# A two-layer encoder on one core: split products of 256 columns put side by side into one of 512, and new lengths in the instruction planner

## The chip, the core and the metric

One core of a Trainium2 chip runs the whole program. The metric is the device time of one execution in microseconds. Engine names are those of the profile: PE multiplies matrices, PEld loads its stationary operand, DVE, ACT and POOL compute on vectors, SP only issues DMAs.

## The reference, cut to what matters

512 tokens of 1024 features pass two layers. Each is a half-step FFN, a mixer, an attention into 256 memory tokens and a second half-step FFN, each followed by a layer norm. The first layer's mixer (even) is dense and windowed attention, the second's (odd) is neighbourhood attention. The change touches the projection of the odd mixer's values and that of the memory's keys:

```
def mixer_c(h, w_in, w_out, rpb):              # the odd mixer
    q, k, v = jnp.split(h @ w_in, 3, axis=-1)
    ...
def memory_attn(h, mem, w_q, w_kv, w_o):
    q = (h @ w_q).reshape(B, S, MEM_HEADS, MEM_HEAD_DIM)
    k, v = jnp.split(mem @ w_kv, 2, axis=-1)
    ...
```

## The kernel before, in words

Products are made in a rounded float type (`fp32r`). To keep fp32's precision each operand is split into a high part (`split`: ACT rounds it by a copy) and a low part (DVE subtracts the high part from the source). `mm3` then adds three products in one PSUM bank: high by high, high by low, low by high. A bank holds 512 fp32 columns per partition.

Two places multiply with a moving operand of only 256 columns, three times for each of eight blocks of 128 features:

- `values` in `mixer_c` (the odd mixer): four groups of 256 columns of `c_w_in`, four blocks of 128 token positions each. The stationary operand is the tokens' features (`xh`, `xl`), the moving one is the weights (`w_cols_k`: two halves of 4 x 256, split into a high and a low slab each). The result is split straight out of PSUM. Group 0 stands at the head of the mixer, where the layer norm of the FFN ahead is still in work; groups 1 to 3 stand between the heads' pairs.
- `keys` in `memory`'s `project`: four heads in each of two layers, two blocks of 128 features. The stationary operand is the weights (`w_cols`), the moving one the memory tokens (`self.mt`, split by `memory_tokens`). Both blocks share a bank, and `split_t2` splits it.

The loop of the odd mixer runs over eight pairs of heads. In it, `queries` and `keys` project, split into two `t2` tiles, and copy the parts by DMAs issued on SP (64 x 512 each, eight for a pair's keys, four for its queries) into slabs that hold both parts on 128 partitions. `weights_of` forms the scores from these slabs in banks `a`, and the softmax. `turned` transposes the weights, `attend` multiplies with the values into banks `d`. The even mixer works alike with `scores` (banks `a`), `turned` (transposes into banks `t`) and `attend`, and has projections to interleave (`last_columns`, `share`).

Nothing is issued as it is written. Each operation goes through `Graph.record` (so the profile gives all of them one line, L154), which notes its dependences and a length from `Graph.cost`. `plan` then lays out all engines in time with these lengths: on each engine the ready operation of the lowest key goes first. `deadlines` takes from that a latest start for DVE, ACT and POOL work, and a second `plan` with these as keys gives the order that is emitted. Tiles come from rings of buffers (`t2` 14, `slab` 27, `raw` 2; PSUM banks `a` 3, `d` 2, `t` 3), granted in the order of recording. So a length in `cost`, or the time at which a buffer comes free, moves instructions on all five engines.

Of the kernel before, what the change touches and what calls it, by code (L numbers as in the profile page):

```python
# [12 lines left out]
F32 = mybir.dt.float32  # L13
F32R = mybir.dt.float32r
# [3 lines left out]
ALU = mybir.AluOpType  # L18
AX = mybir.AxisListType

P = 128
D = 1024
S = 512
NT = S // P
KB = D // P
DFF = 2816
MEM = 256
# [38 lines left out]
class Graph:  # L66
# [45 lines left out]
    @staticmethod  # L112
    def cost(engine, method, out, ins, kw):
        n = 1
        for d in (out if method != "tensor_reduce" else ins[0]).ap[1:]:
            n *= d[1]
        wide = any(z.space == bass.MemoryType.PSUM for z in ins + [out]) if engine != "sync" else False
        if method == "dma_start":
            return 1200.0 if "accum_op" in kw else 600.0
        if engine == "tensor":  # L120
            return max(n / 2.4 + 14, 111)
        scalars = sum(1 for z in ins if z.ap[-1][1] == 1)
        if engine == "vector":
            if method == "tensor_scalar" and not wide:
                n = n / 2
            return n / 0.96 + 72 + 60 * scalars + 120 * (method == "scalar_tensor_tensor" and "accum_out" in kw)
        if engine == "scalar":
            return n / 1.2 + (55 if wide else 100) + 45 * scalars + 130 * ("accum_out" in kw)
        if n <= 8:
            return 270.0 if method == "tensor_scalar" else 200.0 if method != "tensor_tensor" else 390.0 + 157.0 * n  # L130
        if method == "memset":
            return n * 0.83 + 60
        dense = len(ins) == 2 and all(z.ap[-1][0] != 0 for z in ins)
        return n * (2.4 if dense else 1.7) + (70 if dense else 130)
# [182 lines left out]
class Kernel:  # L317
# [81 lines left out]
    def w_cols_k(self, w, c0):  # L399

        src = w[:, c0 : c0 + 256].rearrange("(k p) f -> p k f", p=P)
        half = [lambda r, i=i: r[:, 4 * i : 4 * i + 4, :] for i in range(2)]
        return self.weights([(half[i], half[i](src)) for i in range(2)], (KB, 256), half)

    def w_cols512(self, w, c0):

        got = []
        for q in range(2):
            src = w[q * 512 : (q + 1) * 512, c0 : c0 + 512].rearrange("(k p) f -> p k f", p=P)
            got += self.weights(  # L410
                [(lambda r: r, src)], (4, 512), [lambda r, i=i: r[:, 2 * i : 2 * i + 2, :] for i in range(2)]
            )
        return got
# [800 lines left out]
    def mixer_c(self, ln_i, last):  # L1214
        nc, a = self.nc, self.a
        w_in, w_out = a["c_w_in"], a["c_w_out"]
# [3 lines left out]
        def values(grp, t):  # L1220

            if t == 0:
                wv[0] = self.w_cols_k(w_in, 2 * D + 256 * grp)
                vp[grp] = [self.slab(F32R, (P, 2, 4, 2, 64)) for _ in range(2)]
                if grp == 0:
                    for dst, lo in ((slice(64, 128), 0), (slice(0, 64), 448)):
                        nc.scalar.copy(ends[0][:, :, dst], self.xh[:, :, lo : lo + 64])
                        nc.vector.tensor_copy(ends[1][:, :, dst], self.xl[:, :, lo : lo + 64])
            ps = self.ps("t" if grp else "a")
            for k in range(KB):  # L1230
                mv = [z[:, k % 4, :] for z in wv[0][k // 4]]
                x = self.xT(k, 64 + t * P, 64 + (t + 1) * P) if t < 3 else [z[:, k, :] for z in ends]
                self.mm3(ps[:, :256], x, mv, k == 0, k == KB - 1)
            z = vp[grp][t // 2][:, t % 2]
            self.split(ps[:, :256].rearrange("p (v c) -> p v c", v=4), z[:, :, 0], z[:, :, 1])

        def queries(pair, first=False):

# [121 lines left out]
        vp, qs, ks, acts = {}, {}, {}, []  # L1360
        wv, wq, wk, wo = [None], [None], [None], {}
        for t in range(NT):
            values(0, t)
# [32 lines left out]
    def memory_tokens(self):  # L1396

        raw = self.tile(self.raw, [P, KB, MEM], F32, "raw")
        self.nc.sync.dma_start(out=raw, in_=self.a["mem_t"].rearrange("(k p) m -> p k m", p=P))
        self.mt = []  # L1400
        for kk in range(4):
            self.mt.append(self.split_pair(raw[:, 2 * kk : 2 * kk + 2, :].rearrange("p k m -> p (k m)")))

    def memory(self, i, ln_i, last):
        nc, a = self.nc, self.a
        w_q, w_kv, w_o = a["mem_w_q"][i], a["mem_w_kv"][i], a["mem_w_o"][i]
        memT = lambda k, lo, hi: [z[:, (k % 2) * 256 + lo : (k % 2) * 256 + hi] for z in self.mt[k // 2]]

        def project(head):

            got = {}

            def keys():
                wk = self.w_cols(w_kv, 256 * head)
                ps = self.ps("a")
                for b in range(2):
                    for k in range(KB):
                        self.mm3(ps[:, b * 256 : b * 256 + 256], [z[:, k, :] for z in wk[b]], memT(k, 0, 256), k == 0, k == KB - 1)
                got["k"] = self.split_t2(ps)

            def values():
                wv = self.w_cols512(w_kv, D + 256 * head)
                vs.extend(self.pair() for _ in range(2))
                for m in range(2):
                    ps = self.ps("a")
                    for k in range(KB):
                        self.mm3(ps, memT(k, m * P, (m + 1) * P), [z[:, k % 2, :] for z in wv[k // 2]], k == 0, k == KB - 1)
                    for j, both in enumerate(vs):
                        self.split(ps[:, j * 256 : j * 256 + 256], *(z[:, m * 256 : m * 256 + 256] for z in both))

            def queries(b):
                if b == 0:
                    got["w"] = self.w_cols(w_q, 256 * head)
                ps = self.ps("a")
                for lo, hi in [(0, 256), (256, 512)] if head == 0 else [(0, 512)]:
                    self.project(got["w"][b], ps, lo, hi)
                got["q", b] = self.split_t2(ps, scale=-1.0 / 16)

            return got, [keys] + [values] * (head % 2 == 0) + [lambda: queries(0), lambda: queries(1)]

        def weights_of(kt, q):
            p = []
            for tt in range(2):
                ps = self.ps("a")
                for j in range(2):
                    t = 2 * tt + j
                    for b in range(2):
                        self.mm3(
                            ps[:, j * 256 : j * 256 + 256],
                            [z[:, t * P : (t + 1) * P] for z in q[b]],  # L1450
                            [z[:, b * 256 : b * 256 + 256] for z in kt],
                            b == 0,
                            b == 1,
                        )
                mn = self.small(2, "mn2")
                nc.vector.tensor_reduce(out=mn, in_=ps.rearrange("p (j m) -> p j m", j=2), axis=AX.X, op=ALU.min)
                u = self.t2(F32)
                for j in range(2):
                    c = slice(j * 256, j * 256 + 256)
                    self.softmax(u[:, c], P, mn[:, j : j + 1], 0, 256, sums=ps[:, c])  # L1460
                p.append(u)
            return p
# [20 lines left out]
        acts, hs, out, vs = [], [], [], []  # L1483
        got, todo = project(0)
        for f in todo:
            f()
        for head in range(4):
            p, now = weights_of(got["k"], [got["q", b] for b in range(2)]), vs.pop(0)
            todo = []
            if head < 3:  # L1490
                got, todo = project(head + 1)
            if head == 2:
                out = self.staged(self.down_steps(hs, w_o, 0, 256, 1.0 / ALPHA, [], False, alone=True))
# [135 lines left out]
```

## Time and profile before

| | |
|---|---|
| time before | 2140.82 us, median of 3 runs (2138.66 to 2141.06) |
| the profiled execution's own time | 2139.44 us |
| its span, first to last instruction | 2137.6 us |
| PE, share of the span with a matmul in work | 99%, 12904 matmuls |
| DVE, ACT, POOL, shares of the span | 81%, 54%, 13% |
| granted PE clock | 0.998 |

PE's share counts a matmul until its modelled end, and the next starts earlier: a 256-column matmul stands in the record for 0.28 us, while its successor starts 0.12 us after it. So idle time in the record is smaller than the time lost, and starts of matmuls are compared below. Stages are told by time from the span's start: the even mixer from 346 to 590 us, memory to 700, two FFNs to 1393, the odd mixer to 1600, memory to 1780, the last FFN to the end.

### The profile page before, as it was taken

Reading aid. Unit: us, or ns where it says so; the run is one execution under the profiler, and the core shown is the slowest. Engines: PE = TensorE matmul, PEld = TensorE weight load, DVE = VectorE, ACT = ScalarE, POOL = GpSimd, SP = SyncE. Lnnn points to the kernel's source line nnn. Section 1 sums busy time; section 2 is a strip of 40 time slices with the busy share of each in tenths; the row PEclk is TensorE's granted clock in tenths of the full one; section 3 lists DMA queues with packets and bytes.
Section 4 is the critical chain, followed back from the end, with each engine's and each line's share of the span. In section 5 each row is a group of like instructions: output and inputs, shape, how many; then the busy total and the mean of one; then the engine's idle time right before and its main releaser. Section 6 shows DMA issues by size and latency. Waiting matters only on the chain.

```text
span 2137.6 us, 33130 instructions
## 1 busy us (share of the span) xinstructions
PE 2116.6 (99%) x12904; PEld 1886.3 (88%) x12904; DVE 1725.9 (81%) x2460; ACT 1150.2 (54%) x1863; POOL 288.1 (13%) x379
## 2 busy tenths in 40 slices
PE   9999999999999999999999999999999999999997
PEld 7999988788888899999889999888888888999996
DVE  7789989888748879998879999865568479699997
ACT  5555543798446555445545455456665455445552
POOL 0001015310002000000200000412110011000003
PEclk9999999999999999999999999999999999999999
DMA  6566562003443247564445556255354333456551
GB/s 203 142 165 144 139 188 88 21 17 103 138 138 109 83 115 188 148 153 133 139 108 140 127 139 190 72 168 153 104 163 156 127 102 99 109 148 150 140 155 60
DMA packets 208861, 275.96 MB, mean 129 GB/s; under 512 B 10688, under 2 KB 151616, under 8 KB 208704
## 3 DMA queue, kind: packets, MB, share of 16 engines
q1 hardware_dynamic: 175904, 221.14, 33.3%
q0 software_dynamic: 32512, 52.44, 13.7%
q8 instruction: 102, 1.67, 0.3%
q14 instruction: 55, 0.45, 0.1%
q10 hardware_dynamic: 288, 0.26, 0.0%
HBM read 259.12 MB, written 4.19 MB: 123 GB/s over the span
## 4 chain that ended last, share of the span: by engine, by line
PE 72%; DMA 1%; DVE 1%; ACT 1%; SPq 0%; issue 0%; DVEq 0%; ACTq 0%
PE a L154 45%; PE d L154 15%; PE t L154 11%; DMA slab<-t 1%; DVE slab L154 1%; ACT t L154 0%; DVE x L154 0%; SPq L154 0%; DMA raw<-c_w_in 0%; DMA raw<-ab_w_out 0%; ACT slab L154 0%; DVE t L154 0%; DVE xl L154 0%; ACT junk L154 0%; DVEq L1625 0%
## 5 line engine op out<-in xcount | busy, mean ns | idle before, releaser
L154 DVE TENSOR_TENSOR slab<-slab,slab 128x1024 fp32r<-128x1024 f32 (+3 forms) x638 | 728.6, 1168 | 74.9 <-ACT slab L154 35.8
L154 ACT CAST slab<-slab 128x1024 fp32r<-128x1024 f32 (+2 forms) x498 | 472.3, 983 | 338.9 <-DVE slab L154 141.5
L154 PE MATMUL a<-slab,slab 128*128 128x256 f32 (+2 forms) x2456 | 570.5, 315 | 3.9 <-DMA slab<-t 3.4
L154 PE MATMUL a<-xh,slab 128*128 128x256 f32 (+2 forms) x2480 | 560.2, 315 | 0.1
L154 PEld LDWEIGHTS a<-slab,slab 128*128 128x128 f32 x2456 | 417.2, 191 | 37.4 <-issue 2.7
L154 PE MATMUL d<-slab,slab 128*128 128x512 f32 (+2 forms) x1856 | 447.8, 382 | 0.8 <-DVE slab L154 0.5
L154 PEld LDWEIGHTS a<-xh,slab 128*128 128x128 f32 x2480 | 416.9, 191 | 33.6 <-ACT slab L154 1.0
L154 PE MATMUL a<-xl,slab 128*128 128x256 f32 (+1 forms) x1240 | 390.6, 315 | 0.0
L154 PE MATMUL a<-raw,slab 128*128 128x256 f32 x2048 | 388.9, 283 | 0.9 <-DVE t L154 0.7
L154 PEld LDWEIGHTS d<-slab,slab 128*128 128x128 f32 x1856 | 329.2, 189 | 57.6 <-DVE slab L154 1.2
L154 PEld LDWEIGHTS a<-raw,slab 128*128 128x128 f32 x2048 | 328.1, 192 | 6.4 <-ACT slab L154 1.7
L154 PEld LDWEIGHTS a<-xl,slab 128*128 128x128 f32 x1240 | 236.6, 191 | 18.1
L154 PE MATMUL t<-slab,slab 128*128 128x512 f32 (+1 forms) x864 | 209.6, 383 | 0.0
L154 DVE TENSOR_TENSOR slab<-raw,slab 128x1024 fp32r<-128x1024 f32 (+2 forms) x132 | 158.6, 1220 | 23.7 <-ACT slab L154 23.6
L154 PEld LDWEIGHTS t<-slab,slab 128*128 128x128 f32 x864 | 151.4, 189 | 25.1
L154 DVE TENSOR_TENSOR slab<-t,slab 128x512 fp32r<-128x512 f32 (+2 forms) x211 | 131.4, 642 | 29.0 <-ACT slab L154 27.8
L154 ACT CAST slab<-raw 128x1024 fp32r<-128x1024 f32 (+1 forms) x124 | 123.0, 1021 | 25.7 <-PE a L154 9.0
L154 ACT CAST slab<-t 128x512 fp32r<-128x512 f32 (+2 forms) x211 | 114.4, 567 | 41.5 <-PE t L154 13.7
L154 DVE SCALAR_TENSOR_TENSOR x<-d,x 128x512 f32<-128x512 f32 x168 | 114.8, 686 | 18.8 <-PE d L154 18.0
L154 ACT COPY t<-a 128x512 f32<-128x512 f32 x96 | 56.3, 587 | 125.0 <-PE a L154 71.9
L154 POOL DMA_DIRECT2D slab<-ffn_w_down x40 | 47.7, 1193 | 313.5 <-DVE slab L154 291.2
L154 PE MATMUL a<-slab,xh 128*128 128x512 f32 (+1 forms) x272 | 79.8, 375 | 0.5 <-ACT xh L154 0.5
(126 smaller groups left out, 2138.2 us busy)
## 6 DMA issues: line engine op xcount, KB each, us to landing
slab<-ffn_w_gate SPq DMA_DIRECT2D x80, 512.0 KB
slab<-ffn_w_up SPq DMA_DIRECT2D x80, 512.0 KB
slab<-ffn_w_down SPq DMA_DIRECT2D x80, 512.0 KB
slab<-ffn_w_down POOLq DMA_DIRECT2D x40, 512.0 KB, 5.6
raw<-mem_w_kv SPq DMA_DIRECT2D x16, 1024.0 KB
slab<-t SPq DMA_DIRECT2D x96, 128.0 KB
slab<-ffn_w_gate POOLq DMA_DIRECT2D x16, 512.0 KB, 7.8
slab<-ffn_w_up POOLq DMA_DIRECT2D x16, 512.0 KB, 5.8
```

Of the source, the lines that this page charges most:

```text
L154: op.call = lambda: fn(*args, **kw)
```

## The change

`side_step` puts the high and low parts of the moving operand side by side in one slab: one product of 512 columns with the stationary high part fills both halves of a bank (high by high left, high by low right), and one of 256 columns with the stationary low part adds to the left half. `side_sum` copies the right half out (ACT) and adds the left half (DVE), and the split then reads that sum from a `t2` tile instead of PSUM. `w_cols_side` splits the values' weights in four pieces instead of two; `memory_tokens` writes its parts side by side. The memory's keys take a bank `a` for each block of 128 features instead of one for both. In the planner's `cost`, an operation of DVE or ACT with an operand that starts above partition 0 gets 120 ns more, and one of ACT that is scaled by a tensor 42 ns more.

```diff
         scalars = sum(1 for z in ins if z.ap[-1][1] == 1)
+        aside = 120.0 * any(Graph.extent(z)[0] > 0 for z in ins + [out])
         if engine == "vector":
...
-            return n / 0.96 + 72 + 60 * scalars + 120 * (method == "scalar_tensor_tensor" and "accum_out" in kw)
+            return n / 0.96 + 72 + aside + 60 * scalars + 120 * (method == "scalar_tensor_tensor" and "accum_out" in kw)
         if engine == "scalar":
-            return n / 1.2 + (55 if wide else 100) + 45 * scalars + 130 * ("accum_out" in kw)
+            scaled = 42 * hasattr(kw.get("scale"), "tensor")
+            return n / 1.2 + (55 if wide else 100) + aside + 45 * scalars + 130 * ("accum_out" in kw) + scaled
...
+    def w_cols_side(self, w, c0):
+        raw = self.tile(self.raw, [P, KB, 256], F32, "raw")
+        src = w[:, c0 : c0 + 256].rearrange("(k p) f -> p k f", p=P)
+        for i in range(2):
+            self.nc.sync.dma_start(out=raw[:, 4 * i : 4 * i + 4, :], in_=src[:, 4 * i : 4 * i + 4, :])
+        got = []
+        for q in range(4):
+            got.append(self.slab(F32R, (P, 2, 2, 256)))
+            self.split(raw[:, 2 * q : 2 * q + 2, :], got[q][:, :, 0, :], got[q][:, :, 1, :])
+        return got
+
+    def side_step(self, ps, st, z, k):
+        mm = self.nc.tensor.matmul
+        both = lambda: mm(ps, st[0], z.rearrange("p i n -> p (i n)"), start=k == 0, stop=k == KB - 1, skip_group_check=True)
+        one = lambda: mm(ps[:, :256], st[1], z[:, 0, :], start=False, stop=False, skip_group_check=True)
+        for f in (both, one) if k == 0 else (one, both):
+            f()
+
+    def side_sum(self, dst, ps):
+        self.nc.scalar.copy(dst, ps[:, 256:])
+        self.mix(dst, ps[:, :256], dst, ALU.add)
...
             for k in range(KB):
-                mv = [z[:, k % 4, :] for z in wv[0][k // 4]]
                 x = self.xT(k, 64 + t * P, 64 + (t + 1) * P) if t < 3 else [z[:, k, :] for z in ends]
-                self.mm3(ps[:, :256], x, mv, k == 0, k == KB - 1)
-            z = vp[grp][t // 2][:, t % 2]
-            self.split(ps[:, :256].rearrange("p (v c) -> p v c", v=4), z[:, :, 0], z[:, :, 1])
+                self.side_step(ps, x, wv[0][k // 2][:, k % 2], k)
+            z, y = vp[grp][t // 2][:, t % 2], self.t2(F32)
+            self.side_sum(y[:, :256], ps)
+            self.split(y[:, :256].rearrange("p (v c) -> p v c", v=4), z[:, :, 0], z[:, :, 1])
...
                 wk = self.w_cols(w_kv, 256 * head)
-                ps = self.ps("a")
+                y = self.t2(F32)
                 for b in range(2):
+                    ps = self.ps("a")
                     for k in range(KB):
-                        self.mm3(ps[:, b * 256 : b * 256 + 256], [z[:, k, :] for z in wk[b]], memT(k, 0, 256), k == 0, k == KB - 1)
-                got["k"] = self.split_t2(ps)
+                        self.side_step(ps, [z[:, k, :] for z in wk[b]], self.mt[k // 2][:, k % 2], k)
+                    self.side_sum(y[:, b * 256 : b * 256 + 256], ps)
+                got["k"] = self.split_pair(y)
```

The emitted order is the same through the FFNs' main part and the memory stages on PE; it differs in the even mixer (from about 404 us), at the end of the second layer's first FFN, and in the odd mixer. Two places show how.

On SP, in the odd mixer, around the copies of the keys of pair 3 (pairs are counted from 0; `slab` from `t2`, 64x512) and two loads of weights (`raw`), before:

```order
L154 DMA slab_2597_2678<-t2_2596_2677 64x512 x2
L154 DMA raw_2691_2772<-c_w_in 128x8x256
L154 DMA raw_2758_2839<-c_w_in 128x8x256
L154 DMA slab_2633_2714<-t2_2631_2712 64x512 x2
L154 DMA slab_2633_2714<-t2_2632_2713 64x512 x2
L154 DMA slab_2634_2715<-t2_2631_2712 64x512 x2
L154 DMA slab_2634_2715<-t2_2632_2713 64x512 x2
L154 DMA slab_2651_2732<-t2_2649_2730 64x512 x2
```

The same place now; buffer numbers are shifted (2714 and 2715, the keys, are now 2730 and 2731; the loads are 2790 and 2859):

```order
L156 DMA slab_2611_2692<-t2_2610_2691 64x512 x2
L156 DMA raw_2709_2790<-c_w_in 128x8x256
L156 DMA slab_2649_2730<-t2_2647_2728 64x512 x2
L156 DMA slab_2649_2730<-t2_2648_2729 64x512 x2
L156 DMA slab_2650_2731<-t2_2647_2728 64x512 x2
L156 DMA slab_2650_2731<-t2_2648_2729 64x512 x2
L156 DMA raw_2778_2859<-c_w_in 128x8x256
L156 DMA slab_2667_2748<-t2_2665_2746 64x512 x2
```

The second of the two loads went behind the eight copies of the keys. The same holds two pairs later, where a load of `c_w_out` went behind the eight copies of the keys of pair 5.

On PE, in the even mixer's windowed heads: `t_1032_1113` is a bank of transposes, `a_1036_1117`, `a_1040_1121` and `a_1044_1125` are scores of the head after. Before:

```order
L154 MATMUL t_1032_1113<-ident_1_78,t2_987_1068 128x128
L154 MATMUL t_1032_1113<-ident_1_78,t2_991_1072 128x128
L154 MATMUL a_1036_1117<-slab_858_939,slab_1025_1106 128x256
L154 MATMUL t_1032_1113<-ident_1_78,t2_995_1076 128x128
L154 MATMUL a_1036_1117<-slab_858_939,slab_1025_1106 128x256
L154 MATMUL a_1040_1121<-slab_858_939,slab_1025_1106 128x384 x2
L154 MATMUL a_1044_1125<-slab_858_939,slab_1025_1106 128x384 x2
L154 MATMUL d_1052_1133<-slab_1029_1110,slab_763_844 128x256
```

And now:

```order
L156 MATMUL t_1032_1113<-ident_1_78,t2_987_1068 128x128
L156 MATMUL t_1032_1113<-ident_1_78,t2_991_1072 128x128
L156 MATMUL a_1036_1117<-slab_858_939,slab_1025_1106 128x256 x2
L156 MATMUL a_1040_1121<-slab_858_939,slab_1025_1106 128x384 x2
L156 MATMUL a_1044_1125<-slab_858_939,slab_1025_1106 128x384 x2
L156 MATMUL t_1032_1113<-ident_1_78,t2_995_1076 128x128
L156 MATMUL d_1052_1133<-slab_1029_1110,slab_763_844 128x256
```

Five score matmuls (one of 256 columns, four of 384) went ahead of the bank's last transpose. In two of the dense heads before it, the last bank of transposes likewise has two more score matmuls of 512 columns ahead of it (ahead of `t_799_880`: the second of `a_805_886` and the first of `a_809_890`).

More of the change, by code (lines that the diff above doesn't have):

```diff
@@ L1222, in values @@
             if t == 0:
-                wv[0] = self.w_cols_k(w_in, 2 * D + 256 * grp)
+                wv[0] = self.w_cols_side(w_in, 2 * D + 256 * grp)
                 vp[grp] = [self.slab(F32R, (P, 2, 4, 2, 64)) for _ in range(2)]
@@ L1401, in memory_tokens @@
         for kk in range(4):
-            self.mt.append(self.split_pair(raw[:, 2 * kk : 2 * kk + 2, :].rearrange("p k m -> p (k m)")))
+            z = self.slab(F32R, (P, 2, 2, MEM))
+            self.split(raw[:, 2 * kk : 2 * kk + 2, :], z[:, :, 0, :], z[:, :, 1, :])
+            self.mt.append(z)
     def memory(self, i, ln_i, last):
@@ L1406, in memory @@
         w_q, w_kv, w_o = a["mem_w_q"][i], a["mem_w_kv"][i], a["mem_w_o"][i]
-        memT = lambda k, lo, hi: [z[:, (k % 2) * 256 + lo : (k % 2) * 256 + hi] for z in self.mt[k // 2]]
+        memT = lambda k, lo, hi: [self.mt[k // 2][:, k % 2, i, lo:hi] for i in range(2)]
         def project(head):
```

## The prediction

> **What bounds the kernel now.** I read the page first, then stages, then the starts of single instructions. The page names the engine that the end hangs on:
>
> ```profile
> PE 2116.6 (99%) x12904; PEld 1886.3 (88%) x12904; DVE 1725.9 (81%) x2460; ACT 1150.2 (54%) x1863; POOL 288.1 (13%) x379
> PE 72%; DMA 1%; DVE 1%; ACT 1%; SPq 0%; issue 0%; DVEq 0%; ACTq 0%
> ```
>
> The second line is the chain that ended last: what can be followed of it is PE's. A change pays if it takes time from PE's stream, or takes away a wait in it. Four stages, each with span, then busy time of PE, PEld, DVE, ACT and POOL:
>
> ```profile
> 404.00:540.00 136.00, 132.57 (x741) 110.46 (x741) 112.00 (x285) 122.58 (x286) 15.27 (x45) 1.00 0.20 55
> 590.00:700.00 110.00, 110.00 (x593) 95.31 (x592) 68.40 (x100) 56.90 (x104) 14.82 (x12) 1.00 0.37 116
> 1440.00:1545.00 105.00, 101.55 (x651) 90.49 (x650) 58.01 (x150) 69.47 (x176) 25.18 (x57) 1.00 0.52 137
> 1660.00:1780.00 120.00, 119.97 (x658) 104.12 (x658) 75.96 (x113) 62.24 (x118) 14.83 (x12) 1.00 0.36 110
> ```
>
> In the memory stages (second and fourth) PE never waits. In the mixers (first and third) it waits 3.4 us each, by the record. Those are the only stages of those whose order moves where a reordering can win anything, and the sum has to be made from two kinds of terms: PE's own work, and these waits.
>
> **PE's own work.** The start of a matmul is exact, its end is modelled, so I take the step from one start to the next. A run of 256-column products and one of 512-column products, both three to a block (x2 merges two):
>
> ```profile
> 577.74 0.40 PE L154 MATMUL a<-xh,slab 128*128 128x256 f32 x2
> 577.98 0.28 PE L154 MATMUL a<-xl,slab 128*128 128x256 f32 x1
> ...
> 578.82 0.40 PE L154 MATMUL a<-xh,slab 128*128 128x256 f32 x2
> 594.07 0.39 PE L154 MATMUL a<-xl,slab 128*128 128x512 f32 x1
> 594.30 0.62 PE L154 MATMUL a<-xh,slab 128*128 128x512 f32 x2
> ...
> 595.43 0.39 PE L154 MATMUL a<-xl,slab 128*128 128x512 f32 x1
> ```
>
> Nine products of 256 columns take 578.82 - 577.74 = 1.08 us, 0.120 each; six of 512 take 595.43 - 594.07 = 1.36 us, 0.2267 each. A block now costs 3 x 0.120 = 0.360 us, and later 0.2267 + 0.120 = 0.3467: 0.0133 less. There are 4 groups x 4 token blocks x 8 = 128 such blocks in the odd mixer's values and 2 layers x 4 heads x 2 x 8 = 128 in the memory's keys. 256 x 0.0133 = 3.4 us less. The number of columns streamed is the same; what goes is 256 fixed costs. The starts are rounded to 0.01 us, which leaves 2.4 to 4.4.
>
> The Trainium skill speaks against this: "TensorE: Matmul & The Clock Gate", section "Back-to-back issue gap", gives 262 cycles for 256 columns and 518 for 512, so a merge would save 6 cycles, an estimate of 2.5 ns or 0.6 us over the kernel, and with it the sum below would be -5.9 us. The trace's 0.120 and 0.2267 us are longer than either figure at 2.4 GHz, so here I go by the trace.
>
> **Added work on DVE and ACT.** Each of 16 values blocks and 16 keys blocks adds one 128x256 copy on ACT and one 128x256 addition on DVE, and the values' weights are split in pieces of 512 instead of 1024. The nearest rows (mean ns of one after the count):
>
> ```profile
> L154 ACT CAST slab<-a 128x256 fp32r<-128x256 f32 x20 | 7.5, 373 | 28.3 <-PE a L154 25.6 <-DVE slab L154 2.7
> L154 DVE TENSOR_TENSOR t<-a,slab 128x256 f32<-128x256 f32 x4 | 1.7, 419 | 0.0
> L154 DVE TENSOR_TENSOR slab<-slab,slab 128x512 fp32r<-128x512 f32 x72 | 51.1, 713 | 0.0
> L154 DVE TENSOR_TENSOR slab<-raw,slab 128x1024 fp32r<-128x1024 f32 x116 | 143.9, 1257 | 23.6 <-ACT slab L154 23.6
> ```
>
> On DVE that is 32 x 0.419 = 13.4 us, and 16 x 0.713 - 8 x 1.257 = 1.4 for the splits; on ACT 32 x 0.373 = 11.9. By the stage rows DVE is idle for 42 us of 110 in memory and 47 of 105 in the odd mixer, ACT more than a third of each. A head's keys are ready later by one copy and one addition, 0.8 us; behind them on PE stand the head's queries, 48 products of 0.2267 = 10.9 us, before the scores need them. So I take 0 for all of it. Without that cover it would be 8 heads x 0.8 = 6.4 us.
>
> **The odd mixer's waits.** PE's waits there have one cause:
>
> ```profile
> PE a L154 <- DMA slab<-t: 3.4, 9, 1.2
> PE a L154 <- DMA slab<-t: 2.0, 4, 1.2
> PE a L154 <- DMA slab<-t: 1.1, 3, 0.5
> ```
>
> The first row is the stage (1440 to 1545), the second the scores of pair 3 (1485 to 1493), the third those of pair 5 (1534 to 1539): 7 of 9 waits, 3.1 of 3.4 us. The scores wait for the copies of their keys. What stood ahead of those on SP:
>
> ```profile
> 1477.41 3.25 SPq L154 DMA_DIRECT2D raw<-c_w_in  x2
> 1480.76 9.41 SPq L154 DMA_DIRECT2D slab<-t  x12
> 1486.65 0.40 PE L154 MATMUL d<-slab,slab 128*128 128x256 f32 x2
> 1488.25 0.59 PE L154 MATMUL a<-slab,slab 128*128 128x192 f32 x3 [1.21 <-DMA slab<-t]
> ...
> 1505.46 9.72 SPq L154 DMA_DIRECT2D slab<-t  x12
> 1513.34 0.26 PE L154 MATMUL a<-slab,slab 128*128 128x192 f32 x1
> 1513.79 0.33 PE L154 MATMUL a<-slab,slab 128*128 128x192 f32 x1 [0.20 <-DMA slab<-t]
> ```
>
> Ahead of pair 3's copies two loads of 1 MB are issued; ahead of pair 4's (1505.46) none, and there the loss is one wait of 0.20. The new order puts the second load behind the copies, in both places where PE loses. A recorded wait understates the loss: the matmul ahead of it is drawn for 0.28 us and blocks 0.12, so 0.16 is added to each. Pair 3 loses 2.0 + 4 x 0.16 = 2.6 us, pair 5 1.1 + 3 x 0.16 = 1.6, each undisturbed pair 0.36. If both fall to that, 4.2 - 0.7 = 3.5 us go; the ends are 0 (one load still stands ahead of pair 3's) and 4.8 (all nine). I take 3.4, near the undisturbed pair's row. The loads that were moved back serve queries two pairs on and the output's shares behind those; a pair takes 25 us (from 1480.76 to 1505.46), so nobody waits for them. On POOL memsets and bias additions change places; it is busy for 25 us of 105, and I take 0.
>
> **The even mixer's waits.** The rows of 404 to 540 by what PE writes: 0.8 (d), 0.2 (a) and 2.3 us (t) idle.
>
> ```profile
> L154 PE MATMUL t<-ident,t 128*128 128x128 f32 x210 | 30.1, 277 | 2.3 <-DVE slab L154 1.1 <-ACT t L154 0.9
> 442.30 0.95 PE L154 MATMUL a<-slab,slab 128*128 128x512 f32 x3
> 443.79 0.66 PE L154 MATMUL t<-ident,t 128*128 128x128 f32 x4 [0.54 <-DVE slab L154]
> 503.34 0.36 PE L154 MATMUL a<-slab,slab 128*128 128x256 f32 x1
> 504.65 0.33 PE L154 MATMUL t<-ident,t 128*128 128x128 f32 x1 [0.94 <-ACT t L154]
> 504.73 1.06 PE L154 MATMUL a<-slab,slab 128*128 128x256 f32 x5
> ```
>
> At 504.65 a transpose waits for its softmax: 1.31 us after the start of a product worth 0.12, so 1.19 lost. The five score products that the order now puts ahead of it need about 0.12 + 4 x 0.17 = 0.8 (384 columns taken between the two steps above), and stand ready: before, they ran right behind, from 504.73. At 443.79 about 0.8 is lost, and two products of 512 columns, 0.45, go ahead. Together 1.25 us. The rest of the stage's idle time, about 1.8 us, is made of short waits, of which I count half, 0.9, and 0.15 for what the record hides: -2.3 us. Ends: -4.5 (nearly all) and +2 (as much new waiting as these two).
>
> **The head of the odd mixer.** There PE waits for the layer norm, with group 0 of the values as its filling. 32 of the blocks above lie there, 0.43 us of the saving, and come back as waiting: +0.4.
>
> Sum: -3.4 + 0 - 3.4 - 2.3 + 0.4 = -8.7 us. On the profiled execution (2139.44 us) that gives 2130.7; the median of the runs shown is 1.4 above that execution, so for a median I forecast 2132.1 us.
>
> **Rivals.** *Only PE's own work counts* (16%): in the even mixer ACT is busy for 122.6 of 136 us and may set the pace itself, and the first 1 MB load still stands ahead of pair 3's copies. Then waits move instead of going: -3.4 + 0.4 = -3.0, 2137.8 us. For it: ACT's row. Against: at 504.65 the ready work is there to be seen, and pair 4 shows copies without a load ahead. *The fixed cost isn't won* (6%): a wide product that alternates with a narrow one of another stationary operand could take 0.240 us, since the rows above show each width only among its like; then the first term and the head's go, -5.7, 2135.1 us. The skill's figure would come close to that case. *Slower, by the `t2` ring* (10%): each of the odd mixer's values now takes a `t2` buffer, in the order of recording, ahead of the next pair's tables, exponentials and halves, and holds it for copy, addition and split: two times 0.373 + 0.419, 1.6 us. 12 values stand in the loop. If each holds up the scores behind it for its whole life that costs 19.0 us, +10.3 in all, 2151.1; it turns the sign above 8.7 / 12 = 0.73 us each. For it: the ring is tight, POOL's tables wait for `t2` buffers. Against: in this stage PE waits for nothing but `slab<-t`, so the tables come early enough now.
>
> ```profile
> POOL t L154 <- PE t L154: 40.0, 4, 14.1
> ```
>
> **Chances.** A measurement of this kernel tells about 0.2% from no change, 4.3 us. The forecast's case has 68%; its own range goes from both wait terms at their best (-3.4 - 4.8 - 4.5 + 0.4 = -12.3) to the even mixer at its worst (+2 for -2.3: -4.4), 2128.5 to 2136.4. Faster by over 0.2% takes it and the case of the fixed cost: 0.74. Within 0.2% takes the case of PE's own work: 0.16. Slower: 0.10. For 8 in 10 the range reaches from the forecast's low end to the case of PE's own work: 2128.5 to 2137.8 us.
>
> **What would show it.** Right: 12648 matmuls; steps of 0.347 us a block in values and keys; the memory stages about 0.9 us shorter each, still without waits; near pair 3's and 5's scores one wait of some 0.2 in place of four and three; at the transpose of 504.65 less than 0.5 us lost. Wrong: score matmuls that wait for `t2` tables or for DVE, ACT in the even mixer busy without a gap while PE's waits stay, or blocks that still take 0.36 us.

## The result, and the profile after

The changed kernel takes 2131.07 us, median of 5 runs (2129.74 to 2132.72); the kernel before took 2141.06 beside it (5 runs, 2138.66 to 2142.34). The ratio is 0.9958, its 95% interval 0.9947 to 0.9969, so between 6.6 and 11.3 us are won. The profiled execution took 2131.03 us where that of before took 2139.44: 8.4 us less, against 8.7 worked out. The sum was nearly right; its terms were less so.

From the page of the changed kernel, the engines and the chain that ended last:

```profile
PE 2112.0 (99%) x12648; PEld 1870.6 (88%) x12648; DVE 1735.8 (82%) x2500; ACT 1161.7 (55%) x1903; POOL 285.1 (13%) x379
PE 89%; DVE 1%; DMA 1%; ACT 1%; issue 1%; SPq 0%; DVEq 0%; POOL 0%; ACTq 0%
```

PE has the 256 matmuls fewer and is still the bound. Its 89% of the chain for 72% is in part bookkeeping: the shares of the second line add up to 93%, those before to 75%, the rest could not be followed. The same four stretches by the windows view (span, then PE, PEld, DVE, ACT, POOL), though the program now passes them up to 8 us earlier:

```profile
404.00:540.00 136.00, 134.88 (x760) 113.10 (x759) 114.65 (x292) 124.24 (x289) 13.81 (x45) 1.00 0.20 55
590.00:700.00 110.00, 110.00 (x555) 93.30 (x554) 72.77 (x109) 56.98 (x106) 14.81 (x12) 1.00 0.36 111
1440.00:1545.00 105.00, 103.81 (x587) 88.92 (x585) 62.16 (x157) 75.36 (x194) 25.24 (x58) 1.00 0.52 136
1660.00:1780.00 120.00, 120.00 (x603) 101.70 (x602) 82.23 (x124) 63.62 (x117) 16.30 (x16) 1.00 0.35 106
```

PE's recorded idle time falls from 3.4 to 1.1 us in the even mixer and from 3.4 to 1.2 in the odd one. The memory stages have more DVE work and no waits, as before.

**A block of values.** PE's timeline in the odd mixer, starts first, one wide product (512) and one narrow (256) to a block:

```profile
1441.00 0.40 PE L156 MATMUL t<-slab,xh 128*128 128x512 f32 x1
1441.24 0.28 PE L156 MATMUL t<-slab,xl 128*128 128x256 f32 x1
1441.35 0.39 PE L156 MATMUL t<-slab,xh 128*128 128x512 f32 x1
...
1443.08 0.63 PE L156 MATMUL t<-slab,xh 128*128 128x512 f32 x2
...
1443.78 0.40 PE L156 MATMUL t<-slab,xh 128*128 128x512 f32 x1
...
1445.90 0.40 PE L156 MATMUL t<-slab,xh 128*128 128x512 f32 x1
```

From 1441.00 to 1443.08 are six blocks, 0.347 us each; the six from 1443.78 to 1445.90 take 0.353. In 27 of the 32 groups of eight blocks the trace has all 16 products one behind the other: a block takes 0.347 us in 13 of these groups and 0.352 in 14, 0.349 in the mean. Before, a block took 0.360 in the undisturbed groups of values and keys.

**Where the time went, by stage.** For each matmul that both kernels have, I took its start in the changed kernel minus its start before, and of these the median at each border; the table has what each stage changed. Borders are in us of the kernel before. The first lies at 380 us, as PE's order differs from there on and not only from 404; that of the odd mixer lies behind group 0 of the values. The experiments below were treated alike, each by one profiled execution.

| us | to 380 | even mixer 380-540 | memory, layer 1, 540-1040 | FFNs, head of odd mixer 1040-1407 | odd mixer 1407-1600 | memory, layer 2, to end | sum |
|---|---|---|---|---|---|---|---|
| forecast | 0 | -2.3 | -0.85 | -0.4 + 0.4 | -1.3 - 3.4 | -0.85 | -8.7 |
| changed kernel | -0.11 | -3.49 | -0.83 | -0.36 | -3.18 | -0.47 | -8.4 |
| lengths alone | -0.18 | -3.47 | +0.43 | +0.07 | +2.45 | +0.03 | -0.7 |
| products alone | -0.27 | 0.00 | -0.77 | -0.34 | -0.42 | -0.71 | -2.5 |
| 120 ns only | +0.13 | -2.35 | -0.80 | +0.78 | -1.88 | -0.72 | -4.8 |
| loads moved alone | +0.55 | 0.00 | +0.04 | +0.05 | -3.25 | +0.07 | -2.5 |
| lengths, loads moved | +0.03 | -3.37 | +0.01 | +0.11 | -2.87 | +0.09 | -6.0 |
| two `t2` for a value | +0.21 | -3.26 | -0.75 | -0.36 | +0.50 | -0.28 | -3.9 |
| no `t2` for a value | +0.15 | -3.39 | -0.79 | -0.39 | -3.77 | -0.31 | -8.5 |
| lengths and keys | +1.24 | -3.20 | -0.76 | -0.35 | +2.63 | -0.70 | -1.1 |
| lengths and values | +0.11 | -3.57 | +0.03 | +0.21 | -2.29 | -0.02 | -5.5 |
| copies on two queues | -0.84 | -3.36 | -0.81 | -0.37 | -3.92 | -0.17 | -9.5 |

Up to 380 us PE's order is the same in all of them, so the first column shows how far single executions differ without any cause in the change.

**The even mixer.** The transpose that lost 1.19 us at 504.65 now stands at 501.67, behind six score products, by PE's timeline:

```profile
500.52 1.19 PE L156 MATMUL a<-slab,slab 128*128 128x256 f32 x6
501.67 0.33 PE L156 MATMUL t<-ident,t 128*128 128x128 f32 x1
501.76 0.60 PE L156 MATMUL d<-slab,slab 128*128 128x256 f32 x2
```

The six take 1.15 us from start to start; by the forecast's own steps (two of 0.12, four of 0.17) they need 0.92, so 0.2 is lost there. Some 0.7 us of the stage's gain comes ahead of that, between 400 and 420 us. In the kernel before, a product worth 0.23 us stands 0.63 ahead of the next score there, which waits for ACT; in the changed kernel no such step is left:

```profile
404.81 0.40 PE L154 MATMUL d<-slab,xl 128*128 128x512 f32 x1
405.44 0.50 PE L154 MATMUL a<-slab,slab 128*128 128x512 f32 x1 [0.23 <-ACT t L154]
```

By the groups view of 404 to 540, no transpose of the softmax waits any more, where 2.3 us were idle:

```profile
L156 PE MATMUL t<-ident,t 128*128 128x128 f32 x210 | 30.7, 276 | 0.0
```

**The odd mixer.** SP's timeline, then PE's, at the copies and scores of pairs 3 and 5:

```profile
1475.46 5.62 SPq L156 DMA_DIRECT2D slab<-t  x8
1481.18 0.53 SPq L156 DMA_DIRECT2D raw<-c_w_in  x1
...
1521.20 4.96 SPq L156 DMA_DIRECT2D slab<-t  x8
1526.66 0.37 SPq L156 DMA_DIRECT2D raw<-c_w_out  x1
```

```profile
1482.86 0.58 PE L156 MATMUL a<-slab,slab 128*128 128x192 f32 x3 [0.28 <-DMA slab<-t]
...
1530.38 0.33 PE L156 MATMUL a<-slab,slab 128*128 128x192 f32 x1 [0.60 <-DMA slab<-t]
```

The second load is issued behind the eight copies of a pair's keys, and each place has one wait, with the 0.16 that the record hides 0.44 and 0.76 us. They were 2.6 and 1.6: 3.0 us less. Why the load's place matters stands in the timelines of the kernel before, DVE's and SP's around pair 3, and in SP's waits of 1470 to 1500:

```profile
1477.90 2.35 DVE L154 TENSOR_TENSOR slab<-raw,slab 128x1024 fp32r<-128x1024 f32 x2
1480.28 0.37 SPq L154 DMA_DIRECT2D raw<-c_w_in  x1
SPq L154 <- DMA raw<-c_w_in: 1.6, 1, 1.6
```

SP issues the first load at 1477.41 and the second only at 1480.28, just behind DVE's last split from a `raw` buffer (it ends at 1480.25; the ring has two). At pair 5 it is the same: the split ends at 1528.32, the load is issued at 1528.35. The copies, in order behind it on SP, stand still with it, and one copy of pair 3 waits 1.6 us more for a load to land.

But two losses are new, at the scores of pairs 2 and 6. PE's timeline of the changed kernel:

```profile
1460.50 0.82 PE L156 MATMUL a<-slab,slab 128*128 128x192 f32 x2
1461.16 0.90 PE L156 MATMUL d<-slab,slab 128*128 128x256 f32 x6
...
1552.28 0.33 PE L156 MATMUL a<-slab,slab 128*128 128x192 f32 x1
1552.90 0.33 PE L156 MATMUL a<-slab,slab 128*128 128x192 f32 x1 [0.30 <-DMA slab<-t]
```

And that of the kernel before at pair 2:

```profile
1465.33 0.48 PE L154 MATMUL a<-slab,slab 128*128 128x192 f32 x2
1465.65 0.90 PE L154 MATMUL d<-slab,slab 128*128 128x256 f32 x6
```

Two score products that took 0.32 us to the next start take 0.66 at 1460.50, with no wait in the record, and one takes 0.62 at 1552.28. Against the kernel before, the starts behind these products have slipped by 0.5 us at pair 2 and by 0.65 at pair 6.

### The profile page after: what moved, and what is told of

Its sections match the earlier page's. It is cut to its first block, busy times and chain, and to the rows that moved or that the text cites. A ratio compares the mean times of both kernels' runs of the same rounds, so it can differ in the third digit from the quotient of the medians.

```text
span 2129.3 us, 32714 instructions
## 1 busy us (share of the span) xinstructions
PE 2112.0 (99%) x12648; PEld 1870.6 (88%) x12648; DVE 1735.8 (82%) x2500; ACT 1161.7 (55%) x1903; POOL 285.1 (13%) x379
## 4 chain that ended last, share of the span: by engine, by line
PE 89%; DVE 1%; DMA 1%; ACT 1%; issue 1%; SPq 0%; DVEq 0%; POOL 0%; ACTq 0%
PE a L156 55%; PE d L156 21%; PE t L156 14%; DMA slab<-t 1%; ACT slab L156 1%; DVE slab L156 1%; SPq L156 0%; DVE x L156 0%; ACT t L156 0%; DMA raw<-ab_w_out 0%; DVE t L156 0%; DVE xl L156 0%; DVEq L1657 0%; ACT xh L156 0%; DVE nmu L156 0%
## 5 line engine op out<-in xcount | busy, mean ns | idle before, releaser
L156 PE MATMUL a<-slab,slab 128*128 128x256 f32 (+3 forms) x2320 | 567.6, 323 | 1.9 <-DMA slab<-t 1.2
L156 PEld LDWEIGHTS a<-slab,slab 128*128 128x128 f32 x2320 | 409.4, 190 | 41.7 <-ACT t L156 1.3
L156 DVE TENSOR_TENSOR slab<-t,slab 128x512 fp32r<-128x512 f32 (+2 forms) x223 | 137.5, 637 | 12.3 <-ACT slab L156 11.2
L156 ACT CAST slab<-t 128x512 fp32r<-128x512 f32 (+2 forms) x223 | 120.7, 567 | 41.4 <-DVE t L156 15.0
L156 ACT COPY t<-a 128x512 f32<-128x512 f32 (+1 forms) x116 | 63.5, 551 | 130.0 <-PE a L156 76.5
L156 DVE TENSOR_TENSOR t<-a,t 128x512 f32<-128x512 f32 (+2 forms) x99 | 61.0, 618 | 33.8 <-PE a L156 20.6
```

The costliest lines, as they stand in the source:

```text
L156: op.call = lambda: fn(*args, **kw)
```

## The experiments

Each median stands beside that of the kernel before on the same chip. The intervals are about 2 us to either side, so medians don't tell smaller differences; the stage table does, but for one execution each.

### The two halves of the change

Lengths alone: the kernel before with the new `cost`.

```diff
+        aside = 120.0 * any(Graph.extent(z)[0] > 0 for z in ins + [out])
...
+            scaled = 42 * hasattr(kw.get("scale"), "tensor")
```

> The kernel before with only the planner's new lengths; no product is changed. Theory (the even mixer's gain comes from the lengths, the odd mixer's from the products and the loads' places): the even mixer's waits go as in the changed kernel, about -3.5 us there, the loads on SP stay ahead of the copies of pairs 3 and 5, so the odd mixer keeps its waits, and PE's blocks their 0.36 us: -3 to -4 us in all. Rival (the lengths are only a shuffle, the gain is PE's own work and the loads): within 1 us of before.

Measured 2135.79 us (2135.12 to 2138.82), before 2140.48, ratio 0.998 (0.9971 to 0.9989). The even mixer gains all that it gains in the changed kernel, 3.47 us, and memory gains nothing. In the odd mixer the profiled execution loses 2.45 us. It took 2138.72 us; of the eleven, one other took as long (2138.82) and nine took 2135.12 to 2137.53. So this loss is at the upper end of what the kernel does, and what the odd mixer loses in an execution near the median was not traced. SP's timeline shows both loads still ahead of pair 3's copies, PE's the long waits:

```profile
1473.99 3.24 SPq L156 DMA_DIRECT2D raw<-c_w_in  x2
1477.35 9.94 SPq L156 DMA_DIRECT2D slab<-t  x12
```

```profile
1484.83 0.59 PE L156 MATMUL a<-slab,slab 128*128 128x192 f32 x3 [0.75 <-DMA slab<-t]
1486.86 0.73 PE L156 MATMUL a<-slab,slab 128*128 128x192 f32 x3 [1.08 <-DMA slab<-t]
...
1534.92 0.92 PE L156 MATMUL a<-slab,slab 128*128 128x192 f32 x3 [1.68 <-DMA slab<-t]
```

Products alone: the changed kernel with the old `cost`.

```diff
-        aside = 120.0 * any(Graph.extent(z)[0] > 0 for z in ins + [out])
...
-            scaled = 42 * hasattr(kw.get("scale"), "tensor")
```

> The changed kernel with the planner's old lengths. Theory: PE's blocks save 3.4 us, the loads stand behind the copies as in the changed kernel, the even mixer keeps its waits: -5.5 to -6.5 us. Rival (the lengths carry the odd mixer too): only PE's own work remains, about -3 us.

Measured 2137.0 us (2135.66 to 2141.22), before 2140.48, ratio 0.9988 (0.9979 to 0.9997): near the rival's 3 us, not the theory's 5.5 to 6.5. The even mixer gains nothing, memory nearly what the forecast gives it. In the odd mixer 0.42 us is won, less than PE's own work there, though the loads stand behind the copies here too. By the waits of 1425 to 1560, where the kernel before has 3.4 us in 9:

```profile
PE a L154 <- DMA slab<-t: 2.9, 6, 0.8
```

So the loads' place comes with the products, not with the lengths (by SP's timeline it comes with the values alone and not with the keys alone, below), and with the new products under the old lengths that place is not enough; under the old lengths and products it is (loads moved alone, below).

### One length of the two

The changed kernel without the 42 ns for an operation of ACT that is scaled by a tensor.

```diff
-            scaled = 42 * hasattr(kw.get("scale"), "tensor")
+            scaled = 0 * hasattr(kw.get("scale"), "tensor")
```

> The changed kernel with one of the two new lengths: 120 ns for operands that start above partition 0, without the 42 ns for ACT's scaling by a tensor. The order puts the five score products ahead of the waiting transpose with this length alone. Theory (the partition offset carries the even mixer): even mixer -2.5 to -3.5 us, whole kernel within 1.5 us of the changed kernel. Rival (the 42 ns on ACT, the busiest vector engine there, carry it): even mixer under -1 us.

Measured 2134.69 us (2133.31 to 2137.18), before 2140.14, ratio 0.9977 (0.9968 to 0.9986). The even mixer gains 2.35 us in place of 3.49. A transpose that waits for ACT's softmax is back, by the waits of 430 to 536:

```profile
PE t L156 <- ACT t L156: 0.8, 2, 0.5
```

Both lengths count there, the 120 ns for about two thirds. Against the changed kernel 1.1 us more are lost up to the odd mixer's head, and 1.3 behind it, so the whole is 3.6 us above the changed kernel's median and not within the 1.5 expected.

### The loads behind the copies

The kernel before, its lengths and products unchanged, with the second load put behind the key copies of pairs 3 and 5 on SP by a dependence.

```diff
+                nc.after = (copied[3], {"sync"}) if pair == 6 else None
...
+                nc.after = (copied[5], {"sync"}) if h == 0 else None
```

> The kernel before, old lengths and old products, with only two loads on SP put behind the copies of the keys of pairs 3 and 5 (the planner is told that they wait for those copies; no wait is added on the chip). Theory: the scores of pairs 3 and 5 wait about 0.4 us each instead of 2.6 and 1.6, -2 to -3.5 us. Rival (the copies' own issue on SP, 0.6 us each, sets the wait, and one load still stands ahead): under 1 us.

Measured 2136.55 us (2135.24 to 2137.66), before 2140.48, ratio 0.998 (0.9971 to 0.9989). SP's timeline and PE's waits of 1425 to 1560:

```profile
1481.23 5.36 SPq L154 DMA_DIRECT2D slab<-t  x8
1486.63 0.59 SPq L154 DMA_DIRECT2D raw<-c_w_in  x1
```

```profile
PE a L154 <- DMA slab<-t: 1.2, 3, 0.5
```

The waits fall from 3.4 us in 9 to 1.2 in 3, and 3.25 us are won in the odd mixer and nowhere else. This shows the mechanism by itself, near the size that was forecast.

The same two lines on top of the new lengths:

> The corrected lengths alone, with the second load of 1 MB put behind the key copies of pairs 3 and 5 as in the kernel with only these loads moved; PE's products as before. If the odd mixer's +2.4 to +2.6 us under the lengths alone comes from the loads ahead of those copies, it goes and a gain of about 3.4 us as with the loads alone stands in its place: the stage from 1440 to 1600 us changes by -3 to -3.6, and the median is 2135.79 - 2.6 - 3.4 = about 2130 to 2132 us, like the changed kernel without its new products. The rival, that the loss there is the new order of score products on PE and not the loads, keeps at least half of the +2.5: 2133.5 to 2135.8 us, and waits of over 1 us for the copies stay.

Measured 2134.78 us (2132.86 to 2134.84), before 2140.97, ratio 0.9968 (0.9956 to 0.9981). SP and PE's waits, 1425 to 1560:

```profile
1476.86 5.48 SPq L156 DMA_DIRECT2D slab<-t  x8
1482.39 0.60 SPq L156 DMA_DIRECT2D raw<-c_w_in  x1
```

```profile
PE a L156 <- DMA slab<-t: 1.4, 2, 0.7
```

Between the two traces the odd mixer's loss of 2.45 becomes a gain of 2.87, and no wait of over 1 us is left: in these executions the loss was the loads' place, not the new order of the scores. The median, though, is where the rival put it (2133.5 to 2135.8 us): 6.2 us below before, where the lengths alone are 4.7 below. Between that 1.5 and the traces' 5.3 the worth of the move on top of the lengths stays open, as the profiled execution of the lengths alone lies 2.9 us above its median.

### The `t2` ring

Each value takes one buffer of the ring for copy and sum. Two in place of one, arithmetic unchanged:

```diff
-            z, y = vp[grp][t // 2][:, t % 2], self.t2(F32)
-            self.side_sum(y[:, :256], ps)
+            z, y, by = vp[grp][t // 2][:, t % 2], self.t2(F32), self.t2(F32)
+            self.side_sum(y[:, :256], ps, by[:, :256])
```

> The changed kernel, in which each block of the odd mixer's values takes two t2 buffers instead of one (the copy goes to one, the sum to the other). Theory (the ring isn't what the odd mixer waits for): within 1 us of the changed kernel, about -9 us to before. Rival (the ring holds up scores): each of the 12 calls in the loop costs some tenths of a us more, 3 us or more slower than the changed kernel.

Measured 2134.26 us (2132.0 to 2135.59), before 2140.48, ratio 0.9969 (0.9958 to 0.9981): 3.2 us above the changed kernel's median, at the mark of the rival, though the intervals of the two ratios overlap. In the trace, which is of the longest of the six executions, the odd mixer gives back 3.7, nearly all at pair 7's scores, as PE's timeline shows:

```profile
1575.96 0.33 PE L156 MATMUL a<-slab,slab 128*128 128x192 f32 x1 [1.50 <-DMA slab<-t]
1576.85 0.98 PE L156 MATMUL a<-slab,slab 128*128 128x192 f32 x3 [0.56 <-DMA slab<-t]
```

POOL's waits of 1440 to 1545 show why the ring is short: its tables wait for `t2` buffers that the copies still read. The row in the kernel before, the changed one and this one:

```profile
POOL t L154 <- DMA slab<-t: 12.1, 5, 5.3
```

```profile
POOL t L156 <- DMA slab<-t: 14.0, 6, 4.6
```

```profile
POOL t L156 <- DMA slab<-t: 26.0, 6, 6.8
```

No buffer: the sum goes to one of two fixed places of 256 columns outside the ring.

```diff
-            z, y = vp[grp][t // 2][:, t % 2], self.t2(F32)
+            z, y = vp[grp][t // 2][:, t % 2], self.room[:, 256 * (t % 2) : 256 * (t % 2) + 256]
```

> The changed kernel, in which the sum of the values' halves lies in two fixed places of 256 columns outside the t2 ring (in the tile that takes the layer norm's unused squares), so the odd mixer's values take no t2 buffer, as before the change. Two_t2 lost 3 us to the changed kernel, with a wait of 1.7 us for pair 7's copies. Theory now (one more buffer in the ring moves the order at the mixer's end, the first buffer costs little): 0 to 1 us faster than the changed kernel, the 0.7 us of waits at pair 6's scores gone. Rival (the ring is a steady cost by the buffer): about 3 us faster than the changed kernel, about -12 to before.

Measured 2130.84 us (2130.23 to 2132.69), before 2140.14, ratio 0.9961 (0.9949 to 0.9974): the changed kernel's time. By the starts, the losses at pairs 2 and 6 are gone. Pair 5 gives 0.9 us back: its scores wait 1.2 us in two waits for copies, where the changed kernel waits 0.6 in one. The odd mixer is 0.6 us better in all, which the median doesn't tell.

How a buffer makes scores wait for copies can be read at pair 6. The bias tables lie in `t2` buffers too and are loaded on POOL's queue. In the changed kernel POOL issues these two loads from 1546.48 us on, and by the DMA view of 1547 to 1554 they land 4.5 us later, while SP issues the last two of the keys' copies at 1547.92 and 1548.55:

```profile
t<-bias POOLq DMA_DIRECT2D x2, 128.0 KB, 4.5
```

The kernel before and the one without the buffer have no such row in the same stretch (1556 to 1563 and 1547 to 1554): there the tables have landed before the last copies are issued. That the copies land later for it is argued from these rows; no run moves the tables' loads alone.

### Keys alone, values alone

With the new lengths, the changed kernel with the old values (`w_cols_k`, `mm3`), and with the old keys:

```diff
-                self.side_step(ps, x, wv[0][k // 2][:, k % 2], k)
+                self.mm3(ps[:, :256], x, mv, k == 0, k == KB - 1)
```

> The changed kernel with the old values: side-by-side products for the memory's keys and the new lengths only. On SP the two loads stand ahead of the copies of pairs 3 and 5, as before. Theory: memory -0.8 us a layer, even mixer -3.5, odd mixer about +2.5 as in costs_only: -2.5 us to before. Rival (costs_only's loss in the odd mixer was chance): -5 us.

```diff
-                        self.side_step(ps, [z[:, k, :] for z in wk[b]], self.mt[k // 2][:, k % 2], k)
+                        self.mm3(ps[:, b * 256 : b * 256 + 256], [z[:, k, :] for z in wk[b]], memT(k, 0, 256), k == 0, k == KB - 1)
```

> The changed kernel with the old memory keys: side-by-side products for the odd mixer's values and the new lengths only. Theory: the changed kernel's time less the 1.6 us that its two memory stages win: about -7 us to before, the memory stages as long as before. Rival (the stages hang together by more than PE's work): 3 us or more away from the changed kernel.

Measured 2135.02 us (2133.73 to 2138.89) for keys and 2134.68 (2133.13 to 2136.68) for values, before 2140.14, ratios 0.9982 (0.9974 to 0.9991) and 0.9976 (0.9967 to 0.9985). Keys alone win 0.76 and 0.70 us in the two memory stages and lose 2.63 in the odd mixer, in an execution of 2138.35 us: three of the eleven took 2138.35 to 2138.89, the others 2133.73 to 2135.97. By the median, 5.1 us below before, the rival holds: the odd mixer's loss can't be whole in most executions. Values alone win nothing in memory and 2.29 in the odd mixer, and at 5.5 us below before they miss the 7 expected; they lie 3.6 us above the changed kernel, so by the expectation's mark the stages hang together by more than PE's work. The gain of PE's own work in memory comes with the keys alone, as forecast.

### Half the copies on another queue

The changed kernel, with the copies of the keys' low parts issued by POOL.

```diff
-                for z, part in zip(both, parts):
+                for z, part, q in zip(both, parts, (nc.sync, nc.gpsimd)):
                     for i in range(2):
-                        nc.sync.dma_start(
+                        q.dma_start(
```

> The changed kernel with half of the odd mixer's key copies issued by POOL's queue, not SP's; arithmetic unchanged. If the copies' own issue time on SP (0.62 to 0.78 us each, 8 of them a pair) is what is left of PE's waits there, the eight take about half as long, the 1.2 us of waits for copies and some 0.5 us hidden beside them go: 2129.3 to 2130.5 us. The rival: the copies on POOL wait behind its bias tables and memsets or lengthen them, or the planner's new order costs as much as is won: 2131 us or more, with waits for copies or for tables at the pairs' scores.

Measured 2132.66 us (2130.14 to 2134.17), before 2140.97, ratio 0.9963 (0.9949 to 0.9976). PE's waits of 1425 to 1600:

```profile
PE a L156 <- DMA slab<-t: 1.2, 2, 0.8
```

Nothing that the medians tell is won, as the rival had it, though in the trace the odd mixer is 0.7 us better than the changed kernel's: 1.2 us of waits for copies remain, in two waits. No version tried beats the changed kernel by more than the noise.

## Why the prediction was right, and where it was not

The forecast was 2132.1 us for a median, and 2131.07 came.

**PE's own work (-3.4): right in kind, smaller in size.** A block fell from 0.360 to 0.349 us, over 256 blocks 2.7 us, inside the 2.4 to 4.4 that the rounding left. The memory stages changed by -0.83 and, up to 1780 us, by -0.77, between the 0.68 that 64 such blocks give and the forecast's 0.85. Products alone took 3.5 us off the median (interval 0.6 to 4.5). The rival that the fixed cost isn't won falls with the rows at 1441.00 and 1443.78: a wide product that alternates with a narrow one takes little more than among its like, 0.349 us for both against 0.347. The small saving by "TensorE: Matmul & The Clock Gate", section "Back-to-back issue gap", of the Trainium skill falls too: by an estimate from its isolated gaps 2.5 ns a block were to go, and 10.6 went. By it the head's +0.4 would have shrunk to 0.1 as well, so the forecast's -5.9 for that case should be -6.2.

**Added work on DVE and ACT (0): right.** The memory stages still have no wait.

**The even mixer (-2.3): right in the mechanism, too small.** It came to -3.49, all of it by the lengths (-3.47 alone, nothing without them). The step that was mis-sized is "short waits, of which I count half": the groups view shows all of the transposes' 2.3 us gone, and the 0.7 us won by 420 us lie ahead of both places that the forecast named. The rival that ACT sets the pace falls: ACT is busy 124.24 of 136 us and PE's waits went all the same.

**The odd mixer's waits (-3.4): mechanism shown, sum too large.** At pairs 3 and 5 3.0 us went where 3.5 were counted, and with the loads moved alone 3.25. The step that failed is that nothing else in this stage would change: its 96 blocks of values give 1.0 us of the stage's 3.2, so the waits gave 2.2 and not 3.4. New losses of 0.5 and 0.65 us at pairs 2 and 6 make up most of the difference. Both are gone when the values leave the `t2` ring, so the values' buffers set them, in this order; without the buffers pair 5 loses 0.9 us instead. Nor is the loads' place enough in every order: products alone have it, and 2.9 of the 3.4 us of waits remain. Which moved instruction takes the gain back there was not settled.

**The head (+0.4): right.** From 1300 us to 1407, behind group 0, the starts moved by 0.02, so what group 0's blocks save came back there. Of waits the record has only 0.2 us more.

**The rival of the `t2` ring (10%, 2151.1 us): a true mechanism at a small price.** One buffer a value cost about 1.1 us in two places, not 19.0; without it the odd mixer is 0.6 us better in all and the median the same. A second buffer cost 3.2 us by the medians, whose intervals overlap. Both are far from the 8.7 us that turn the sign.

**Terms counted at nothing.** Before 380 us 0.11 went, less than single executions differ there (-0.84 to +1.24). Between 1040 and 1300 0.38 went, in every kernel with the new keys and in none without; there the kernel before has one wait of PE, which the changed one lacks:

```profile
PE a L154 <- ACT slab L154: 0.2, 1, 0.2
```

The even mixer's excess of 1.2 us and these cover what the odd mixer (1.5) and the second memory stage (0.4) fell short. That the sum is nearer than its terms is luck.

## What to carry to other kernels

A merge of two narrow products into a wide one saves the fixed cost of one matmul, to be read as a step between starts, and only where the engine never waits. When the order comes from a planner, other lengths can be worth as much as a change of the arithmetic, and the two should be tried apart and together: here lengths alone won 4.7 us by the medians, products alone 3.5, and both 10.0. Whether the new lengths win because they are truer, or because any other order might have lost those waits, was not tested. A gain from a wait that goes has to be searched for at the neighbours too, since a buffer ring can give part of it back. And copies that stand behind a load on an in-order queue wait for that load's buffer too.

## What was not expected of the hardware

A matmul of 512 columns that alternates with one of 256, with another stationary operand each time, takes 0.347 to 0.352 us for both, where the two widths among their like take 0.347: the alternation costs almost nothing. Copies of 64 x 512 take SP 0.62 to 0.70 us each to issue (4.96 and 5.62 us for eight in the changed kernel), so one pair's keys keep the queue for 5 to 6 us. A load that has to wait for its buffer holds the copies behind it as long (2.4 us at pair 3 before).
